# A hybrid decoder layer: early window transfers and gate projections dealt over the sample units

## The chip, the cores and the metric

The kernel runs on one core of a Trainium2 chip. The metric is the device time of one execution in microseconds, the median of the runs shown. TensorE (PE) does the matrix products, ScalarE (ACT) and VectorE (DVE) the element-wise work, GpSimd (POOL) some element-wise work and the issue of gathers, SyncE (SP) the issue of most transfers.

## The reference

One inference step of a decoder layer for a prompt of 512 tokens and a batch of 8 single-token samples with 2048 past positions. What matters here, cut down:

```python
h = rms_norm(x, ln1_g)
u2, q, kc, vc, ks, vs, kw, vw, ng, g_conv, g_attn = split(h @ w_in)      # D_MODEL = 1024
u = u2[..., :1024] * sigmoid(u2[..., 1024:])
c_out = silu(layer_norm(depthwise_conv(u, width=31))) @ w_conv_pw
# attention: 16 heads, 4 key/value heads; three branches, each softmax(q k - alibi) v, weighted by gates from ng:
#   compressed blocks; 16 selected blocks of 64 rows; sliding window of 512 rows
# prompt: causal over 512 tokens. sample: 2048 cached rows in pages (cache_slc_kv), 512 rows of state_win_kv
m = sigmoid(g_conv) * c_out + sigmoid(g_attn) * a_out
x = x + m @ w_out
x = x + square(relu(rms_norm(x, ln2_g) @ w_up)) @ w_down
y = rms_norm(x, lnf_g)
```

The outputs are the layer's result for prompt and samples and the updated key/value and convolution state.

## The kernel before

Prompt and samples are worked on together: activations lie transposed, 128 channels by 520 columns (512 prompt tokens and 8 samples), in two halves of 256 and 264 columns. Each matrix product is done as three matmuls of split operands, high by high, high by low and low by high, so a projection tile of 128 output channels costs 8 x 3 x 2 = 48 matmuls in `dense` (L435 to L437). `wload` fetches its weights in two pieces of 256 KB over SP's queue (L400) into three rotating raw buffers, casts the high part on ACT (L412) and subtracts for the low part (L414).

The work goes in stages. First come the norm, projections and prompt attention (`attend`, to about 500 us). Beside it run the pooled past of the samples (`pool_cache`, buffers `cg`), the convolution (`conv_taps`, L1099 on DVE) and first projections (`u_proj`) as fillers. Then comes the sample stage (`Sample`), then the merge with `w_conv_pw` (`merge`, beside `residual`, which loads x again), then the output projection and the feed-forward part to the end.

The sample stage has ten columns of two units each, in the order of SORDER: columns 8 and 9 are the sliding window of samples 0 to 3 and 4 to 7, columns 0 to 7 the selected past of one sample each. A unit reads two row sets (tile `sg`, 128 x 2048 numbers, 1 MB each): a window transfer from `state_win` (L900) or a gather (L317), both issued on POOL. A unit transposes its rows (L925), copies them on ACT (L926), forms scores (L929), takes them over on DVE (L934) and ACT (L936), transposes them (L938), multiplies them with the values (L941) and copies the result (L944). Six `sg` buffers rotate, so a row set can be fetched once the unit three back is through L941. They lie in memory that prompt attention gives free. `finish` joins the units; its large product is L1013.

Gate projections run beside this as fillers: `gate_attn` (eight tiles, the first during prompt attention) and `gate_conv` (eight tiles). From the second on, an attention gate may go as soon as prompt attention has been written out; conv gates 0 to 5 follow, and gates 6 and 7 (HELD) are held until the last unit's scores (L929) are issued. A hold is `issue_after`: the matmuls stand behind the named instruction in TensorE's order.

The order on each engine is fixed when the program is built. Generators write instructions in the ratio of their weights (`run`; W_S for the sample units, W_D2 for the gates), with a priority (`urgent` raises it, `lowered` lowers it). A planner, which simulates a time line, then puts on each engine the ready instruction of highest priority. An engine then works in that order: what waits holds up all that stands behind it on its engine, and so does a transfer on SP's or POOL's queue. Memory is given out in areas from the left and from the right; a tile waits for the tiles that lay there before.

In `residual` (L1463) the loads of x go to an area on the right that takes over memory of the sample stage; the loads of the merge's weights follow on the same SP queue.

Of the kernel before, what the change touches and what calls it, by code (L numbers as in the profile page):

```python
# [17 lines left out]
P = 128  # L18
# [12 lines left out]
EPS = 1e-6  # L31
FILL = 3000
TL_S = True
KTS_B, SG_B, U1, Y1, UP1 = 5, 6, 2, 4, 4
SC_D = (1, 2)
PS1 = {"pss": 2, "pst": 2, "pso": 1, "psp": 1}
PS2 = {"psx": 2, "psy": 3, "psn": 1}
# [18 lines left out]
U_EARLY = (32, 48, 56, 74)  # L56
POOL_P, PROJ_D = True, False
GA1, W_G, PRI_G = 1, 2, 500
W_P, W_D, W_S, W_D2, W_C, W_U = 55, 55, 120, 8, 300, 20
WIN_E = lambda nc: nc.gpsimd  # L60
XF = False
LOW_D = 6
# [1 line left out]
SQ_D, WARM, EARLY = (), 20, 2  # L64
NORDER = "q0 q1 s02 m0 m1 t0 t1 q2 q4 q3 s25 m4 m2 t4 m3 t2 t3"
PACK = 5000
HELD = 6
SYNC = mybir.DependencyInfo(mybir.DependencyClass.Sync, mybir.DependencyReason.DATA)
BIG = 1e30
FLOOR = 1e25  # L70
# [60 lines left out]
def hybrid_layer(ctx: ExitStack, tc: tile.TileContext, I, C, O):  # L131
# [297 lines left out]
    def dense(wh, wl, aH, aL, evac, n=P, ins=None, halves=(0, 1)):  # L429
        for hf in halves:  # L430
            c = HS[hf]
            ps = psd()[:, :c.stop - c.start]
            for k in range(KD):
                with after(ins):
                    pe.matmul(ps[:n], wh[:, k, :n], aH[:, k, c], start=(k == 0), stop=False)  # L435
                pe.matmul(ps[:n], wh[:, k, :n], aL[:, k, c], start=False, stop=False)  # L436
                end = pe.matmul(ps[:n], wl[:, k, :n], aH[:, k, c], start=False, stop=(k == KD - 1))  # L437
            ends.append(end)
            evac(hf, c, ps)
# [434 lines left out]
    class Sample:  # L874
# [10 lines left out]
        def first(self):  # L885
# [4 lines left out]
            dve.tensor_copy(self.sn.rearrange("p s b -> p b s"), ps)  # L890
            yield

        def cached(self, b, q):
            g = self.gp.tile([P, 4, 512], F32, name="sg", bufs=SG_B)
            gather(cache_s, gix[:, b, q:q + 1], g)
            return g

        def window(self, b):
            g = self.gp.tile([P, 4, 512], F32, name="sg", bufs=SG_B)
            WIN_E(nc).dma_start(g, state_win[b].rearrange("(p r) f -> p r f", r=4))  # L900
            return g

        def attend(self, col):
# [8 lines left out]
            for e in range(2):  # L912
# [3 lines left out]
                for i in range(2):  # L916
# [4 lines left out]
                    for h in range(2):  # L921
                        kt = sp.tile([P, 512], F32, name="kts", tag="kts", bufs=KTS_B)
                        ps = psx([P, 4, P])
                        for r in range(4):
# [3 lines left out]
                    yield  # L928
                run_ = packed([lambda n=n: pe.matmul(pq[32 * n:32 * n + 32], Qz[:, n % 2, bs[n // 2]], kts[n], start=True, stop=True,  # L929
                                              skip_group_check=True) for n in range(4)], *cps)  # L930
                if col == SORDER[-1] and e == 1:
                    UY["scored"] = run_
                t = sp.tile([P, 512], F32, name="tq", tag="kts", bufs=KTS_B)
                dve.tensor_tensor_reduce(out=t, in0=pq, in1=bias.rearrange("p r k -> p (r k)"), scale=1.0,  # L934
                                         scalar=FLOOR, op0=OP.add, op1=OP.min, accum_out=st[:, 0, at:at + 1])
# [283 lines left out]

    def gate_attn():  # L1220
        for k in range(KD):
            while ("attn", k) not in built or (k >= GA1 and "late" not in UY):
                yield
            wh, wl = wload(w_in, [(C_GA + P * k, P)])
            ga = temp("ga")

            def ev(hf, c, ps):
                act.activation(ga[:, c], ps, AF.Tanh, scale=0.5)
                p0, n = pcols(hf)
                a = attnT[:, k, p0:p0 + n]  # L1230
                dve.scalar_tensor_tensor(a, ga[:, p0:p0 + n], 1.0, a, op0=OP.add, op1=OP.mult)
            dense(wh, wl, hH, hL, ev)
            dve.tensor_scalar(sA[:, k], ga[:, NP_:], 1.0, None, op0=OP.add)
            yield

    def gate_conv():
        for k in range(KD):
            while k >= HELD and "scored" not in UY:
                yield
            wh, wl = wload(w_in, [(C_GC + P * k, P)])  # L1240
            gc = GC[k] = gcp.tile([P, T], F32, name="gc", bufs=KD)
            dense(wh, wl, hH, hL, lambda hf, c, ps: act.activation(gc[:, c], ps, AF.Tanh, scale=0.5),
                  ins=UY["scored"] if k >= HELD else None)
            yield

    def merge(cH, cL, mH, mL):
# [117 lines left out]
    def pool_conv():  # L1364
        yield from pool_cache(plp2)
        last = UY["cs"]
        for b in range(NB):
            with tc.issue_after(last.ins):
                last = nc.sync.dma_start(o_win_s[0, b, 0:511].rearrange("l j h d -> l (j h d)"), state_win[b, 1:512])
            yield  # L1370
        pl2_s.close()
        while NKV - 1 not in KV:
            yield
        UY["mo"], mo = area("mo", side="right")
        UY["msk"], UY["oC"] = mo.tile([P, NB, 32], F32, name="msk"), mo.tile([P, 2, 256], F32, name="oC")
        cs, cp_ = area("cmpp", side="right")
        yield from urgent(sample_cmp(cp_, UY["msk"], UY["oC"]), PRI_C)
        cs.close()
# [75 lines left out]
    m2s, m2 = area("m2")  # L1454
    mH = m2.tile([P, KD, T], F32R, name="mH")
    mL = m2.tile([P, KD, T], F32R, name="mL")
    gs, gp = area("gp", side="right")

    def residual():
        for j in range(5):  # L1460
            n = P if j < 4 else NB
            xt = gp.tile([P, D], F32, name="xr", tag="p4", bufs=2)
            nc.sync.dma_start(xt[:n], xp[P * j:P * j + P] if j < 4 else xs)  # L1463
            for kk in range(2):
                ps = pst([P, 4, P])
                for k in range(4):
                    c = (4 * kk + k) * P
                    pe.transpose(ps[:, k, :n], xt[:n, c:c + P], ident[:n, :n])
                act.copy(x1[:, 4 * kk:4 * kk + 4, P * j:P * j + n], ps[:, :, :n])
            yield  # L1470
    run((merge(cH, cL, mH, mL), 8), (residual(), 4))
    gs.close()
    gc_s.close()
    UY["st"].close()
    UY["mo"].close()
    uy1_s.close()
    xgH = hp.tile([P, KD, T], F32R, name="xgH", tag="H")
# [160 lines left out]
```

## Time and profile before

| | us |
|---|---|
| median of 3 runs | 1187.1 |
| lowest and highest run | 1181.41, 1187.92 |
| the profiled execution, its time | 1196.35 |
| the profiled execution, its span | 1194.5 |
| TensorE busy in the span | 1135.8 (95%) |
| VectorE busy | 747.4 (63%) |
| ScalarE busy | 542.6 (45%) |
| GpSimd busy | 253.0 (21%) |

The profile is one execution. The page gives each engine's busy time in the span; matmuls overlap, so a busy TensorE is one that has work, and its idle time is read from the windows. The granted clock is the share of full speed that TensorE was given, a mean over the stretch of its two levels, 1.2 and 2.4 GHz. "Idle before" in brackets is the time an engine stood before an instruction and what released it.

### The profile page before, as it was taken

To read this page: it belongs to the slowest core of one execution; us is meant where nothing else is said; L and a number is where in the kernel's file an instruction comes from. 1 tells how busy PE (TensorE), PEld (TensorE's weight loads), DVE (VectorE), ACT (ScalarE), POOL (GpSimd) and SP (SyncE) were. 2 spreads that over 40 slices of the span, in tenths; PEclk is the share of its full clock that TensorE was granted. 3 is DMA by queue.
4 is the path that set the end of the run, shared out by engine and by line. 5 is a ranking of instruction groups with operands and counts; after the bars stand their busy time and mean duration, and the time that the engine had idled before them with its cause. 6 is when DMAs were issued, how large, how long until landed. Compare 5 with 4: busy or idle time off the path is not lost.

```text
span 1194.5 us, 24755 instructions
## 1 busy us (share of the span) xinstructions
PE 1135.8 (95%) x9755; PEld 1006.2 (84%) x9755; DVE 747.4 (63%) x1773; ACT 542.6 (45%) x1384; POOL 253.0 (21%) x284
## 2 busy tenths in 40 slices
PE   6899998999999999999999699999999999999996
PEld 6777974776677677888898579999999999999996
DVE  4341455486899799989976666556543443443476
ACT  5352465535542655345657734344431431431454
POOL 2345445343474012003322300000000000000012
PEclk9899999999998999999999999999999999999998
DMA  6646555173364851657787624333333333333354
GB/s 175 179 135 206 166 150 168 39 209 99 115 177 118 292 153 37 203 199 251 281 304 270 221 89 126 89 89 107 90 98 97 89 89 89 97 98 90 89 166 136
DMA packets 188364, 175.46 MB, mean 147 GB/s; under 512 B 35277, under 2 KB 171021, under 8 KB 182984
## 3 DMA queue, kind: packets, MB, share of 16 engines
q1 hardware_dynamic: 172472, 96.54, 28.5%
q0 software_dynamic: 15296, 76.55, 18.4%
q8 instruction: 77, 1.26, 0.4%
q10 hardware_dynamic: 480, 0.79, 0.3%
q14 instruction: 39, 0.32, 0.1%
HBM read 167.58 MB, written 14.80 MB: 153 GB/s over the span
## 4 chain that ended last, share of the span: by engine, by line
PE 73%; DVE 13%; DMA 8%; issue 2%; ACT 2%; POOL 1%; SPq 1%; DVEq 0%; ACTq 0%; POOLq 0%
PE psd L435 18%; PE psd L436 18%; PE psd L437 18%; DVE y L1099 5%; DMA wraw<-in_w_in_dram 3%; PE psx L925 3%; PE psp L772 3%; DMA sg<-in_cache_slc_kv_dram,gix 2%; PE pss L679 2%; DMA cg<-in_cache_cmp_kv_dram,gic 2%; PE pso L744 2%; PE pst L739 2%; DVE pp L643 2%; DVE pp L728 2%; PE psy L941 2%
## 5 line engine op out<-in xcount | busy, mean ns | idle before, releaser
L412 ACT CAST wh<-wraw 128x512 fp32r<-128x512 f32 x282 | 162.3, 617 | 296.4 <-PE psd L436 219.6
L435 PE MATMUL psd<-hH,wh 128*128 128x264 f32 (+2 forms) x848 | 249.9, 296 | 4.4 <-ACT hH L348 2.2
L437 PE MATMUL psd<-hH,wl 128*128 128x264 f32 (+2 forms) x848 | 245.7, 292 | 0.2 <-POOL wl L414 0.2
L436 PE MATMUL psd<-hL,wh 128*128 128x264 f32 (+2 forms) x848 | 245.0, 290 | 0.4 <-DVE hL L349 0.4
L414 DVE TENSOR_TENSOR wl<-wraw,wh 128x512 fp32r<-128x512 f32 (+1 forms) x230 | 154.5, 707 | 77.5 <-ACT wh L412 73.2
L1099 DVE SCALAR_TENSOR_TENSOR y<-u,cwT,y 128x512 f32<-128x512 f32 x240 | 192.7, 803 | 4.5
L435 PEld LDWEIGHTS psd<-hH,wh 128*128 128x128 f32 (+1 forms) x848 | 160.5, 190 | 13.5 <-issue 7.1
L437 PEld LDWEIGHTS psd<-hH,wl 128*128 128x128 f32 (+1 forms) x848 | 159.9, 189 | 7.8 <-issue 6.6
L436 PEld LDWEIGHTS psd<-hL,wh 128*128 128x128 f32 (+1 forms) x848 | 160.6, 190 | 4.5 <-issue 3.2
L435 PE MATMUL psd<-xgH,wh 128*128 128x264 f32 (+1 forms) x512 | 144.8, 283 | 0.0
L436 PE MATMUL psd<-aT,wh 128*128 128x264 f32 (+1 forms) x512 | 144.7, 283 | 0.0
L435 PE MATMUL psd<-aT,wh 128*128 128x264 f32 (+1 forms) x512 | 144.7, 283 | 0.0
L437 PE MATMUL psd<-aT,wl 128*128 128x264 f32 (+1 forms) x512 | 144.7, 283 | 0.0
L437 PE MATMUL psd<-xgH,wl 128*128 128x264 f32 (+1 forms) x512 | 144.5, 282 | 0.0
L436 PE MATMUL psd<-xgL,wh 128*128 128x264 f32 (+1 forms) x512 | 144.2, 282 | 0.0
L1577 POOL TENSOR_TENSOR attnT<-attnT,gfb 128x512 f32<-128x512 f32 (+1 forms) x8 | 10.5, 1331 | 493.7 <-DVE sqd L1572 493.7
L647 ACT ACTIVATE pp<-pp,st 128x256 f32<-128x256 f32 (+3 forms) x128 | 71.2, 557 | 84.1 <-DVE st L643 77.3
L436 PEld LDWEIGHTS psd<-xgL,wh 128*128 128x128 f32 x512 | 96.6, 189 | 0.0
L437 PEld LDWEIGHTS psd<-xgH,wl 128*128 128x128 f32 x512 | 96.5, 188 | 0.0
L435 PEld LDWEIGHTS psd<-aT,wh 128*128 128x128 f32 x512 | 96.3, 188 | 0.1
L435 PEld LDWEIGHTS psd<-xgH,wh 128*128 128x128 f32 x512 | 96.3, 188 | 0.0
L436 PEld LDWEIGHTS psd<-aT,wh 128*128 128x128 f32 x512 | 96.2, 188 | 0.0
(380 smaller groups left out, 2262.3 us busy)
## 6 DMA issues: line engine op xcount, KB each, us to landing
wraw<-in_w_in_dram SPq DMA_DIRECT2D x88, 256.0 KB
wraw<-in_w_down_dram SPq DMA_DIRECT2D x80, 256.0 KB
wraw<-in_w_up_dram SPq DMA_DIRECT2D x64, 256.0 KB
sg<-in_state_win_kv_dram POOLq DMA_DIRECT2D x8, 1024.0 KB
out_dram<-in_state_win_kv_dram SPq DMA_DIRECT2D x8, 1022.0 KB
wraw<-in_w_in_dram SPq DMA_DIRECT2D x32, 128.0 KB
wraw<-in_w_conv_pw_dram SPq DMA_DIRECT2D x16, 256.0 KB
wraw<-in_w_out_dram SPq DMA_DIRECT2D x16, 256.0 KB
```

The source lines that it names most:

```text
L412: act.copy(a, raw[:, :, :o])
L414: (low or (dve if 2 <= len(loaded) < LOW_D else LOW[0])).tensor_tensor(b, raw[:, :, :o], f32(a), op=OP.subtract)
L435: pe.matmul(ps[:n], wh[:, k, :n], aH[:, k, c], start=(k == 0), stop=False)
L436: pe.matmul(ps[:n], wh[:, k, :n], aL[:, k, c], start=False, stop=False)
L437: end = pe.matmul(ps[:n], wl[:, k, :n], aH[:, k, c], start=False, stop=(k == KD - 1))
L643: v = dve.tensor_tensor_reduce(out=ph, in0=ps, in1=bias, scale=slope[e], scalar=FLOOR, op0=OP.add, op1=OP.min, accum_out=st[:, 0, e, i:i + 1])
L647: act.activation(ph, ph, AF.Exp, scale=-1.0, bias=st[:, 0, e, i:i + 1], accum_out=st[:, 1, e, i:i + 1])
L679: mms.append(lambda ps=ps, e=e, i=i, xi=xi, nk=nk: pe.matmul(ps, rq(e, i), KR[g, e, r][:, 32 - xi:32 + nk], start=True, stop=True))
L728: dve.tensor_scalar(ph, ph, rr[:, e, i:i + 1], None, op0=OP.mult)
L772: packed([lambda r=r, j=j, i=i: pe.matmul(po[32 * i:32 * i + 32, j], wpa[:, 2 * rh + r, j], gs[i][:, r, 256 * j:256 * j + 256], start=(rh ...
L925: pe.transpose(ps[:, r], g[:, r, P * h:P * h + P], ident)
L1099: prev = dve.scalar_tensor_tensor(yk, u[:, w:w + NP_], cwT[:, k, w:w + 1], yk, op0=OP.mult, op1=OP.add)
```

## The change

- Two of the six `sg` buffers go, and a new area `sgx` of three such buffers is opened on the right, after the pooled past is done, in memory that its tiles (`cg` and others) have left: seven buffers in all. The windows of samples 0, 1 and 2 are fetched into it at that place in the program, before `sample_cmp`. `rows` then takes three row sets from `sgx` and four from the old area in turn.
- The area stays until the merge is done, and `residual` loads x into it (three buffers) in place of an area of its own.
- The memory for DMA descriptors goes from 16384 to 8192 bytes, which makes room for 8 KB more per partition.
- Every unit's last score matmul is kept in `UY["scored", n]`. Attention gate k (k from 1) is held until unit GA_AT[k] is scored, and conv gate k until unit GC_AT[k]. The hold for the end (HELD) goes.
- The generator weight W_D2 of the gates goes from 8 to 40.

```diff
-KTS_B, SG_B, U1, Y1, UP1 = 5, 6, 2, 4, 4
+SGX, KTS_B, SG_B, U1, Y1, UP1 = 3, 5, 4, 2, 4, 4
-W_P, W_D, W_S, W_D2, W_C, W_U = 55, 55, 120, 8, 300, 20
+W_P, W_D, W_S, W_D2, W_C, W_U = 55, 55, 120, 40, 300, 20
-HELD = 6
+GA_AT, GC_AT = (0, 1, 3, 5, 7, 8, 9, 10), (11, 12, 13, 14, 15, 16, 17, 18)
...
+        def rows(self):
+            self.n = n = getattr(self, "n", SGX - 1) + 1
+            if n % (SGX + SG_B) < SGX:
+                return UY["sgx"].tile([P, 4, 512], F32, name="sg", tag="sgx", bufs=SGX)
+            return self.gp.tile([P, 4, 512], F32, name="sg", bufs=SG_B)
+
         def cached(self, b, q):
-            g = self.gp.tile([P, 4, 512], F32, name="sg", bufs=SG_B)
+            g = self.rows()
             gather(cache_s, gix[:, b, q:q + 1], g)
...
         def window(self, b):
-            g = self.gp.tile([P, 4, 512], F32, name="sg", bufs=SG_B)
+            if UY["pre"]:
+                return UY["pre"].pop(0)
+            g = self.rows()
...
-                if col == SORDER[-1] and e == 1:
-                    UY["scored"] = run_
+                UY["scored", 2 * SORDER.index(col) + e] = run_
...
     def gate_attn():
-            while ("attn", k) not in built or (k >= GA1 and "late" not in UY):
+            while ("attn", k) not in built or (k >= GA1 and ("scored", GA_AT[k]) not in UY):
...
-            dense(wh, wl, hH, hL, ev)
+            dense(wh, wl, hH, hL, ev, ins=UY["scored", GA_AT[k]] if k >= GA1 else None)
...
     def gate_conv():
-            while k >= HELD and "scored" not in UY:
+            while ("scored", GC_AT[k]) not in UY:
...
-                  ins=UY["scored"] if k >= HELD else None)
+                  ins=UY["scored", GC_AT[k]])
...
+        sgx_s, UY["sgx"] = area("sgx", side="right")
+        UY["sgx_s"], UY["pre"] = sgx_s, []
+        for b in range(SGX):
+            g = UY["sgx"].tile([P, 4, 512], F32, name="sg", tag="sgx", bufs=SGX)
+            WIN_E(nc).dma_start(g, state_win[b].rearrange("(p r) f -> p r f", r=4))
+            UY["pre"].append(g)
         cs, cp_ = area("cmpp", side="right")
...
-    gs, gp = area("gp", side="right")
...
-            xt = gp.tile([P, D], F32, name="xr", tag="p4", bufs=2)
+            xt = UY["sgx"].tile([P, 4, 512], F32, name="xr", tag="sgx", bufs=SGX).rearrange("p r f -> p (r f)")[:, :D]
...
-    nc = bacc.Bacc("TRN2", target_bir_lowering=False, num_devices=1, dynamic_dma_scratch_size=16384)
+    nc = bacc.Bacc("TRN2", target_bir_lowering=False, num_devices=1, dynamic_dma_scratch_size=8192)
```

## Rows read from the trace of the kernel before

**Rows 1.** Stages: length, PE, PEld, DVE, ACT, POOL, PEclk, DMA share, GB/s.

```profile
430.00:500.00 70.00, 68.98 (x573) 55.48 (x571) 67.73 (x183) 32.33 (x98) 10.83 (x16) 1.00 0.31 87
500.00:510.00 10.00, 10.00 (x110) 9.66 (x106) 8.40 (x15) 3.78 (x8) 1.75 (x4) 1.00 0.89 318
510.00:530.00 20.00, 18.23 (x154) 15.32 (x157) 14.88 (x28) 8.22 (x19) 0.46 (x1) 0.91 0.42 138
530.00:590.00 60.00, 59.38 (x659) 53.34 (x649) 57.63 (x102) 34.89 (x79) 22.13 (x26) 1.00 0.78 264
590.00:660.00 70.00, 69.27 (x762) 60.91 (x761) 47.74 (x87) 44.99 (x100) 20.01 (x21) 1.00 0.82 283
660.00:690.00 30.00, 21.03 (x244) 14.37 (x243) 19.62 (x38) 20.87 (x41) 6.84 (x6) 0.89 0.56 206
690.00:710.00 20.00, 18.45 (x218) 15.49 (x217) 11.54 (x63) 4.73 (x11) 0.00 (x0) 1.00 0.32 107
710.00:720.00 10.00, 9.38 (x57) 8.60 (x58) 8.36 (x16) 6.44 (x14) 0.00 (x0) 0.83 0.35 105
800.00:900.00 100.00, 100.00 (x834) 99.84 (x834) 55.24 (x114) 41.59 (x89) 0.00 (x0) 1.00 0.33 96
```

**Rows 2.** Waits of TensorE, 440 to 720 us: total us, times, longest.

```profile
PE psx L925 <- DMA sg<-in_cache_slc_kv_dram,gix: 8.0, 5, 2.8
```

**Rows 3.** Chain that ended last, 498 to 725 us: start us, us, what.

```profile
502.48 13.38 DMA wraw<-in_w_in_dram
...
560.84 6.46 DMA sg<-in_cache_slc_kv_dram,gix
...
583.97 0.99 PE psy L929 x8
584.97 1.03 PE psx L925 x8
...
586.35 1.01 PE psy L941 x32
...
675.91 8.03 DMA sg<-in_cache_slc_kv_dram,gix
...
704.73 4.25 DMA wraw<-in_w_conv_pw_dram
```

**Rows 4.** Time line of POOL: start us, us, engine, line, what, idle before.

```profile
439.91 2.10 POOL L730 TENSOR_SCALAR pp<-pp,st 128x128 f32<-128x128 f32 x4 [14.62 <-DVE st L655]
...
477.01 0.61 POOL L900 DMA_DIRECT2D sg<-in_state_win_kv_dram  x1
...
499.66 2.09 POOL L900 DMA_DIRECT2D sg<-in_state_win_kv_dram  x4 [3.74 <-PE pso L744]
...
539.82 1.02 POOL L317 DMA_INDIRECT sg<-in_cache_slc_kv_dram,gix  x1 [7.89 <-PE psy L941]
```

**Rows 5.** DVE's time line: scores of units 0, 7, 18, 19; convolution's last step.

```profile
521.99 0.69 DVE L934 CUSTOM_DVE_ANT_0 tq<-psy,sb_win 128x512 f32<-128x512 f32 x1
...
585.43 0.68 DVE L934 CUSTOM_DVE_ANT_0 tq<-psy,bm 128x512 f32<-128x512 f32 x1
...
678.07 0.69 DVE L934 CUSTOM_DVE_ANT_0 tq<-psy,bm 128x512 f32<-128x512 f32 x1
...
687.38 0.70 DVE L1210 SCALAR_TENSOR_TENSOR y<-th,v 128x520 f32<-128x520 f32 x1 [1.31 <-ACT th L1205]
689.38 0.69 DVE L934 CUSTOM_DVE_ANT_0 tq<-psy,bm 128x512 f32<-128x512 f32 x1 [1.30 <-PE psy L929]
```

**Rows 6.** ACT's time line: attention gates 1 and 2 end; merge's weights.

```profile
478.30 0.38 ACT L1228 ACTIVATE ga<-psd 128x264 f32<-128x264 f32 x1
...
508.98 0.39 ACT L1228 ACTIVATE ga<-psd 128x264 f32<-128x264 f32 x1
...
708.25 1.36 ACT L412 CAST wh<-wraw 128x512 fp32r<-128x512 f32 x2 [3.16 <-DMA wraw<-in_w_conv_pw_dram]
```

**Rows 7.** Waits of SP's queue, 640 to 740 us.

```profile
SPq L1463 <- PE psy L1013: 46.1, 1, 46.1
```

More of the change, by code (lines that the diff above doesn't have):

```diff
@@ L1471, in hybrid_layer @@
     run((merge(cH, cL, mH, mL), 8), (residual(), 4))
-    gs.close()
     gc_s.close()
     UY["st"].close()
+    UY["sgx_s"].close()
     UY["mo"].close()
```

## The prediction

> **What bounds the kernel now.** I read the page first (TensorE is busy for nearly the whole span), then the busy time by stage to see where it is not. The stages before 430 us and after 720 us are left alone by the change: in the feed-forward stage TensorE is busy 100.00 of 100 us at full clock with 834 matmuls, 0.120 us each [rows 1]. So a microsecond counts only if TensorE stands or runs slow between 430 and 720 us. The same rows give that ledger as stretch minus busy time: 1.0 us lost in 430 to 500, 0 in 500 to 510, 1.8 in 510 to 530, 0.6 in 530 to 590, 0.7 in 590 to 660, 9.0 in 660 to 690, 1.6 in 690 to 710 and 0.6 in 710 to 720: 15.3 us of idle. Below full clock the loss is (1 - granted clock) times the stretch: 0.09 x 20 = 1.8, 0.11 x 30 = 3.3 and 0.17 x 10 = 1.7, together 6.8 us. All that any change here can win is 22 us.
>
> The waits of TensorE say what the 9.0 us are: its transposes of sample rows (L925) wait 8.0 us for gathered row sets [rows 2]. The fillers had run out; the last row set takes 8.03 us in the chain [rows 3]. A second hole, at 515 us, is a weight load that took 13.38 us [rows 3], issued 3 us after four 1 MB window transfers had been issued in one go at 499.66 [rows 4].
>
> **Prices.** A projection tile is 3 x 8 x 2 = 48 matmuls: 48 x 0.120 = 5.8 us [rows 1], and 0.52 MB of weights. A sample unit (half a column, two row sets, 20 units in all) is, by the chain's pieces, two groups of L925 at 1.03, L929 at 0.99, L941 at 1.01 [rows 3], and L938 with half a group's transposes, 0.5: 4.6 us.
>
> **The early windows.** Three of eight window transfers leave the stretch after 477 us and go to where the pooled-cache tiles have been read for the last time. The data rate of 430 to 500 us is 87 GB/s, share 0.31 [rows 1], so 3.1 MB fit in. Three issues at about 0.6 us [rows 4] go into POOL's queue ahead of the scalings of prompt attention (L730); POOL stands idle 14.62 us before one of these [rows 4], so 1.8 us costs nothing; if a window were queued there before its memory is free, the scalings behind it wait too, up to the few us until that memory is read. I take 0, between -1 and 5.
> The Trainium skill, "SBUF — State Buffer", section "A bandwidth-pool intuition that's wrong", says that a transfer issued by GpSimd can stretch from about 620 to 3100 ns beside DVE copies, because descriptors wait for a shared port. Worked out from that figure, an estimate: 2.5 us more per row set. DVE is busy 67.73 of 70 us in 430 to 500 and 57.63 of 60 in 530 to 590 [rows 1], yet a gather there took 6.46 us where the last one, with DVE two thirds busy, took 8.03 [rows 3]: the trace does not show it. By the rule the 13 row sets up to unit 7 could take up to 32 us more, which is the slower rival (c); by the rows, nothing.
> What the early windows bring: the first unit, scored at 521.99 [rows 5], can start when prompt attention frees the PSUM banks, about 500, so it is scored near 507. Fewer windows are in flight beside the 13.38 us weight load: its stall and the low clock behind it (1.8 + 1.8 us) mostly go.
>
> **Seven row buffers for six.** A unit's gathers wait for L941 three units back; with seven, one of the two waits for four back. Worth a little slack, priced at 0. The descriptor memory halves; before, at most six row sets were in flight, after it seven. No row shows a full descriptor memory; the nearest is the issue itself, four in 2.09 us without a pause [rows 4]. I take 0; the far end is that each of 40 issues doubles, 40 x 0.5 = 20 us on a POOL that is idle two thirds of the stretch [rows 1], so at most a few us reach TensorE; a gain has no way to come from it.
>
> **The dealt gates.** The generator's weight (W_D2, 8 to 40) only sets how soon a gate is written into the program behind its unit and adds no instruction: 0. Two attention gates (k = 1 and 2), which filled TensorE until 478.30 and 508.98 [rows 6], are now held until units 1 and 3 are scored: 11.6 us of filler leaves the stretch up to 509. The last pair of first-projection tiles can move up into it (11.6 us), if its buffers allow. From 500 to the score of unit 7 TensorE then has 8 x 4.6 = 37, gates 1 to 3 = 17, half of the last pair = 6: 60 us. The transfers of that stretch are 13 row sets and about six tiles, 13.6 + 3.1 = 16.7 MB; at the 283 GB/s of 590 to 660 [rows 1] that is 59 us from 499, then about 6 us from landing to score: 564. At 264 GB/s it is 568, at 318 (500 to 510) 558 [rows 1]. I take 565 for the score of unit 7 (585.43 before [rows 5]), with 6 us of TensorE idle instead of 0.6.
> From there each unit has one gate beside it (k = 4 to 7 of attention, then conv 0 to 6): 11 x (4.6 + 5.8) = 114 us, plus some 6 for the convolution's sums, which interleave: unit 18 is scored at about 685, against 678.07 [rows 5], but with two more gates done. Per unit 2.6 MB in 10.4 us is 250 GB/s, below the 283 already sustained, so no gather should be waited for: 9.0 us of idle and 3.3 us of clock go, about 1 us stays.
>
> **The tail.** Before, two conv gates (11.6 us) were kept for the end; the last unit is scored at 689.38 [rows 5] and the merge starts behind the weight cast of 708.25 [rows 6], near 710. After, only conv gate 7 is left, about half of it for the tail. What is late next is the merge's weights. SP had the residual's loads (L1463) ahead of them, and they waited 46.1 us for L1013, the last product of the sample stage [rows 7]. Now the residual's rows lie in the window buffers, freed a unit or two earlier, and the merge's weights wait only for the last unit's L941. I put that 5 us after the score (reading 0.69, exponent, transpose, copy, product), and the load with casts at 4.25 [rows 3] + 1.36 [rows 6] + some 2 for issue and subtraction. So the merge starts 12.6 us after the last score, of which TensorE has about 4.5 us of its own and 3 of gate 7: 5 us idle, and about 2 us of low clock after it. The convolution's last step ends at 687.38 + 0.70 [rows 5], and its split needs some 5 us more: 693, not the bound.
>
> **Sum.** Lost after: 1 (430 to 500) + 6 (to unit 7) + 1 (to unit 18) + 5 (tail) + 0.5 (elsewhere) + 2 (clock) = 15.5; before 22.1: a gain of 6.6. By times instead: last score near 688 (unit 18 at 685 plus about 4.6, less overlap), merge at 701 against 710, a gain of 9, and 1.5 more if its first tile does not repeat 1.7 us of low clock: 10.5. I take the middle, 8.6 us. The profiled execution has a span of 1194.5 in 1196.35 us; it would become 1187.8. The runs' median lies 9.25 lower; the same difference puts it at 1187.1 - 8.6 = **1178.5 us**.
>
> **Rivals.** (a) *TensorE alone bounds the early units.* If the row sets come at 318/0.89 = 357 GB/s, the rate of 500 to 510 at full share [rows 1], they are there by 546 and unit 7 is scored at 500 + 60 = 560: 5 us better, 1173.5. Against it: no stretch of 60 us shows more than 283. Chance 0.15.
> (b) *The hole moves.* The last first-projection pair cannot take the place of the held gates, because its output buffer waits for DVE's convolution and DVE is 97% busy there [rows 1]; TensorE then idles 5.8 us for gate 1 and some 2 for gate 2 before 509. The gain falls to 8.6 - 7.8: 1186.3. For it: DVE's load. Against it: only the last write of such a tile needs that buffer. Chance 0.25.
> (c) *Slower: the early units stay gather-bound.* Place: units 0 to 7, which have three gates instead of about five for filler. If TensorE, which works in a written order, stands before transposes whose rows are late, and unit 7 is scored at its old 585.43, then 11 gates still come behind it: 585 + 120 + the last unit, and the merge starts 20 us later than forecast, 11 later than before: 1198. It decides from unit 7 later than 565 + 9 = 574; every us behind that is a us lost. For it: each unit needs 2.1 MB in 8 us, 263 GB/s beside weights, about what 530 to 590 shows at share 0.78 [rows 1]. Against it: the windows' head start of 3 MB. Chance 0.18.
> (d) *The windows do not come early* (POOL takes them where it did before): unit 0 starts near 515 with the gates still held; about half of (c): 1190. Against it: POOL's idle [rows 4]. Chance 0.07.
> The forecast has the remaining 0.35, with 1174 to 1184 as its own range.
>
> **Range and chances.** About 0.5%, 6 us, is what a measurement of this kernel tells from no change: faster means below 1181.2, slower above 1193.0. Forecast (nearly 0.3 of 0.35) and (a) give faster 0.46, and a twelfth of the rest 0.03: 0.49. (c) gives most of slower, 0.14, and (d) and the unknown ends of POOL's queue 0.04: 0.18. The same: 0.33. The range runs from 1169, half of the remaining idle gone, to 1195, most of (c).
>
> **What would show it.** Right: window transfers on POOL before 450 us; unit 0 scored before 510 and unit 7 before 570; no wait above 1 us of L925 for gathers after 600; the residual's loads no longer waiting for L1013; merge at about 701 with a hole of some 5 us ahead of it. Wrong: idle TensorE between 450 and 510 (b), L925 waiting for gathers in 510 to 570 (c), or a merge that waits for the convolution.

## The result, and the profile after

The changed kernel took 1194.18 us in the median of 7 runs (1192.1 to 1196.75), the kernel before 1187.92 in 7 runs beside it (1181.41 to 1192.92): ratio 1.0064, 95% interval 1.0041 to 1.0088. It is slower by 6.3 us; 1178.5 was forecast. The profiled execution has a span of 1192.4 us. The ratios below leave out three single executions that ran far slower than their neighbours (1380.72 us in e2, 6131.11 in e4, and 3627.24 in e9, its profiled one); the medians of these three kernels are over all runs and lie 0.1 to 0.3 us higher for it.

The stages of the changed kernel, with the columns of [rows 1]:

```profile
430.00:500.00 70.00, 59.63 (x479) 38.96 (x478) 65.80 (x174) 32.93 (x97) 13.64 (x21) 0.90 0.35 123
500.00:510.00 10.00, 10.00 (x111) 9.07 (x110) 3.52 (x7) 4.44 (x11) 2.36 (x3) 1.00 0.90 335
510.00:530.00 20.00, 20.00 (x236) 17.95 (x238) 9.36 (x21) 12.07 (x28) 4.88 (x5) 1.00 0.82 287
530.00:590.00 60.00, 60.00 (x664) 54.98 (x657) 58.07 (x93) 34.37 (x77) 20.07 (x19) 1.00 0.80 277
590.00:660.00 70.00, 70.00 (x792) 61.05 (x791) 49.11 (x111) 40.66 (x91) 16.29 (x22) 1.00 0.74 250
660.00:690.00 30.00, 29.66 (x283) 26.66 (x283) 24.00 (x71) 15.57 (x31) 0.00 (x0) 1.00 0.39 103
690.00:710.00 20.00, 15.26 (x125) 15.05 (x124) 17.72 (x31) 13.01 (x25) 0.00 (x0) 0.97 0.21 62
710.00:720.00 10.00, 10.00 (x77) 10.00 (x77) 6.89 (x14) 5.35 (x11) 0.00 (x0) 0.88 0.18 51
```

From 500 to 690 TensorE is idle for 0.3 us, where [rows 1] shows 12 us. The part that the windows were to mend is mended. But 430 to 500, which had 68.98 of 70 at clock 1.00 [rows 1], now has 59.63 at a granted clock of 0.90: 10.4 us idle and 6 us of slow clock. And 690 to 710 is still short by 4.7 us.

GpSimd's time line of the changed kernel (start, duration, what): the windows do go out early, and the first gather goes out at 497.87 instead of 539.82 [rows 4].

```profile
421.37 0.61 POOL L1387 DMA_DIRECT2D sg<-in_state_win_kv_dram  x1
433.13 1.06 POOL L1387 DMA_DIRECT2D sg<-in_state_win_kv_dram  x2 [11.15 <-issue]
497.87 1.18 POOL L317 DMA_INDIRECT sg<-in_cache_slc_kv_dram,gix  x1 [0.30 <-PE psy L945]
```

VectorE's time line, the scores of units 0, 7, 18 and 19 and the convolution's last step; they answer to [rows 5]:

```profile
490.01 0.69 DVE L941 CUSTOM_DVE_ANT_0 tq<-psy,sb_win 128x512 f32<-128x512 f32 x1
547.65 0.69 DVE L941 CUSTOM_DVE_ANT_0 tq<-psy,bm 128x512 f32<-128x512 f32 x1
643.23 0.68 DVE L941 CUSTOM_DVE_ANT_0 tq<-psy,bm 128x512 f32<-128x512 f32 x1
651.10 0.68 DVE L941 CUSTOM_DVE_ANT_0 tq<-psy,bm 128x512 f32<-128x512 f32 x1
712.38 0.70 DVE L1217 SCALAR_TENSOR_TENSOR y<-th,v 128x520 f32<-128x520 f32 x1
```

The last unit is scored 38 us earlier than in [rows 5], the convolution's last step comes 25 us later (30 earlier and 32 later than in the second profile of the kernel before, e1 below; the first was late ahead of this stage). What happened to the convolution stands in ScalarE's time line, where each dense product is read out (tb and ah are the two products of a first projection, ga an attention gate):

```profile
444.38 0.38 ACT L1064 ACTIVATE tb<-psd 128x264 f32<-128x264 f32 x1
499.91 0.39 ACT L1235 ACTIVATE ga<-psd 128x256 f32<-128x256 f32 x1 [0.87 <-PE psd L437]
507.83 0.39 ACT L1057 ACTIVATE ah<-psd 128x256 f32<-128x256 f32 x1
509.81 1.14 ACT L412 CAST wh<-wraw 128x512 fp32r<-128x512 f32 x2 [1.11 <-PE psd L436]
510.86 0.38 ACT L1235 ACTIVATE ga<-psd 128x264 f32<-128x264 f32 x1
```

After projection 4 (444.38) no dense product is read out for 55 us. Then gate 1 comes (499.91), and only behind it projection 5 (507.83), though no hold is on projection 5. The order in which a pair of weight tiles and an accumulator bank are handed out is the order in the source: gate 1, projection 5, gate 2, projection 6, gates 3 to 5, projection 7. There are two pairs and two banks. Gate 1 takes a pair and both banks (one for each half), and it may start only behind unit 0, which needs the end of prompt attention. So in the trace gate 1 begins on TensorE at 494.32, behind the last product of prompt attention (done at 483.9), and projection 5 behind gate 1, at 503.40. In the kernel with the row sets alone (e4 below) gate 1 begins at 439.2 and projection 5 at 451.39, between the attention products, the last of which is done at 493.9.

SyncE's queue stands as well: it issues four pieces of weights from 433.20 to 446.8 and the next at 511.18, where the kernel with the row sets alone issues twelve between 431 and 488. First a small constant (L883) waits 32.2 us for memory of prompt attention, then the weight load behind it 30.7 us until an earlier one has been split (L414), which needs a free weight tile (total us, times, longest):

```profile
SPq L400 <- DVE wl L414: 74.9, 6, 30.7
SPq L883 <- DVE pt L742: 32.2, 1, 32.2
```

The queue is not what held projection 5 back. The weights of its first product were cast and split by 446.4, and no other weights were cast before 509.81; its first matmul still ran at 503.40, behind gate 1:

```profile
443.35 1.12 ACT L412 CAST wh<-wraw 128x512 fp32r<-128x512 f32 x2
445.14 1.27 DVE L414 TENSOR_TENSOR wl<-wraw,wh 128x512 fp32r<-128x512 f32 x2
503.40 0.37 PE L435 MATMUL psd<-hH,wh 128*128 128x256 f32 x1
```

TensorE's own waits in 430 to 500 name none of this:

```profile
PE pst L739 <- POOL pp L730: 3.3, 3, 1.8
PE pst L739 <- ACT pt L742: 2.2, 2, 2.0
PE pso L744 <- DVE pt L742: 2.0, 3, 0.9
```

These are prompt attention's own steps (mask, copy, normalise). They ran before too, but with dense work between them TensorE waited 1.0 us for them there (e1); that work is what is gone. A hole of this kind is not found under the wait that it shows, but under the work that is missing there.

Late projections make late taps (the convolution's multiply-and-add steps on VectorE), and the merge waits at its start. The first merge product of the changed kernel:

```profile
709.35 0.58 PE L435 MATMUL psd<-cH,wh 128*128 128x256 f32 x1 [4.74 <-ACT gc L1249]
```

It waited for the last conv gate's read-out (gc), which ScalarE did at 708.91, behind some of the convolution's tanh and split (cH) steps. That the late convolution makes this wait is not shown: e12 below waits 5.2 us at the same place with its convolution done at 681.

### The profile page after: what moved, and what is told of

Same layout as the page of the kernel before. It is cut to its first block, busy times and chain, and to the rows that moved or that the text cites. A ratio compares the mean times of both kernels' runs of the same rounds, so it can differ in the third digit from the quotient of the medians.

```text
span 1192.4 us, 24768 instructions
## 1 busy us (share of the span) xinstructions
PE 1134.0 (95%) x9755; PEld 1006.5 (84%) x9755; DVE 745.4 (63%) x1773; ACT 545.7 (46%) x1384; POOL 249.9 (21%) x284
## 4 chain that ended last, share of the span: by engine, by line
PE 75%; DVE 11%; DMA 8%; ACT 2%; issue 2%; POOL 1%; SPq 1%; DVEq 0%; POOLq 0%; ACTq 0%
PE psd L435 19%; PE psd L436 19%; PE psd L437 19%; DVE y L1106 5%; DMA cg<-in_cache_cmp_kv_dram,gic 4%; PE psx L933 3%; DMA wraw<-in_w_in_dram 3%; PE psp L772 2%; PE pss L679 2%; PE psy L948 2%; PE psy L937 2%; PE pso L744 2%; PE pst L739 2%; DVE pp L643 1%; DVE pp L728 1%
## 5 line engine op out<-in xcount | busy, mean ns | idle before, releaser
L414 DVE TENSOR_TENSOR wl<-wraw,wh 128x512 fp32r<-128x512 f32 (+1 forms) x230 | 155.0, 711 | 96.3 <-ACT wh L412 92.2
L1106 DVE SCALAR_TENSOR_TENSOR y<-u,cwT,y 128x512 f32<-128x512 f32 x240 | 196.4, 818 | 4.9
```

Source lines behind the costliest of these rows:

```text
L414: (low or (dve if 2 <= len(loaded) < LOW_D else LOW[0])).tensor_tensor(b, raw[:, :, :o], f32(a), op=OP.subtract)
L1106: prev = dve.scalar_tensor_tensor(yk, u[:, w:w + NP_], cwT[:, k, w:w + 1], yk, op0=OP.mult, op1=OP.add)
```

## Experiments

Theory 1, from the traces above: a held attention gate closes the rotation of weight tiles and banks to the projections behind it; TensorE loses its filler in prompt attention, the convolution is late, the merge waits. Against it: the seven row sets and early windows cost by themselves (rival 2); sixteen dealt gates leave too little filler or too much for the end (rival 3); the new order of the weight tiles costs, held or not (rival 4); the halves of the change hurt only together (rival 5).

Ratios are to runs of the kernel before on the same chip, with 95% intervals. Behind the ratios stands a sum from each kernel's one profiled execution: the idle time of TensorE in 430 to 720, and what it lost to a granted clock below 1 (busy time times 1 minus the clock, in the eight stretches of [rows 1]). "Read-out" is when ScalarE first reads out projection 4's second product (tb), a common mark at the start of the stretch; "rest" is the execution's time less read-out, idle and clock.

| kernel | median us | ratio, interval | profiled us | read-out | idle | clock | rest |
|---|---|---|---|---|---|---|---|
| before, first profile | 1187.9 | | 1196.35 | 441.66 | 15.3 | 5.5 | 733.9 |
| before, second profile (e1) | 1188.3 | | 1188.30 | 435.43 | 16.4 | 2.9 | 733.5 |
| changed | 1194.2 | 1.0064 (1.0041 to 1.0088) | 1194.18 | 437.72 | 15.5 | 7.6 | 733.4 |
| e4 row sets alone | 1180.2 | 0.9928 (0.9903 to 0.9954) | 1180.03 | 435.83 | 6.4 | 3.4 | 734.4 |
| e7 dealing alone | 1205.7 | 1.0138 (1.0110 to 1.0167) | 1205.70 | 433.97 | 25.0 | 12.4 | 734.4 |
| e5 row sets, one hold | 1200.8 | 1.0113 (1.0089 to 1.0136) | 1203.90 | 441.19 | 19.9 | 7.0 | 735.8 |
| e10 changed, gate 1 free | 1187.8 | 0.9997 (0.9975 to 1.0019) | 1186.04 | 435.50 | 9.7 | 5.8 | 735.0 |
| e6 changed, no attention holds | 1181.2 | 0.9938 (0.9915 to 0.9962) | 1185.26 | 441.51 | 5.9 | 4.4 | 733.5 |
| e2 changed, projections first | 1181.2 | 0.9934 (0.9909 to 0.9959) | 1178.81 | 433.16 | 7.3 | 5.0 | 733.4 |
| e11 the same, gates free | 1181.0 | 0.9936 (0.9911 to 0.9962) | 1179.60 | 434.52 | 5.8 | 2.9 | 736.3 |
| e3 gates free, handed out fast | 1186.3 | 0.9975 (0.9956 to 0.9995) | 1183.25 | 438.68 | 14.1 | 1.5 | 728.9 |
| e12 gates free, handed out slowly | 1188.5 | 0.9984 (0.9954 to 1.0015) | 1188.50 | 437.24 | 12.6 | 3.9 | 734.7 |
| e8 third weight pair | 1195.6 | 1.0063 (1.0042 to 1.0083) | 1196.65 | 435.24 | 17.6 | 12.0 | 731.8 |

The last column stays within 732 to 736 (729 in e3) while the profiled times spread over 27 us: where two executions differ, they differ by TensorE time in this stretch, or by a shift ahead of it. Such a shift cannot be put down to an edit: the two profiles of the kernel before differ by 6.2 us there.

**e1, the kernel before again** (no edit).

> The kernel before, unchanged, for a second profile. The first one ended some 9 us above the median of its times and was already 3.9 us late at 400 us, where both kernels run the same work; this one should end near 1188, with the first merge matmul near 704 to 706 instead of 710.19 and everything between 430 and 690 as in the first profile, shifted by about 4 us. If it ends near 1196 again, the first profile stands as it is and the two traces can be laid on one another without a shift.

1188.3 us, span 1186.5; its merge starts at 702.60, and 430 to 500 has 69.03 of 70 at clock 1.00. 6.2 of the 7.6 us by which the first profile's merge was later (710.19) lie ahead of the stage. The changed kernel's merge start (709.35) is 6.8 us later than here, of which 2.3 lie ahead of the stage (read-out) and 4.5 in it.

```profile
430.00:500.00 70.00, 69.03 (x599) 56.77 (x596) 66.55 (x176) 31.14 (x95) 12.54 (x19) 1.00 0.36 106
660.00:690.00 30.00, 22.88 (x269) 18.18 (x268) 19.79 (x67) 17.54 (x35) 4.80 (x5) 0.94 0.39 141
702.60 0.39 PE L435 MATMUL psd<-cH,wh 128*128 128x256 f32 x1 [2.15 <-ACT cH L1216]
```

Idle time and clock loss together are 1.0 us here and 16.3 in the changed kernel in 430 to 500, 14.2 and 0.3 in 500 to 690, 4.1 and 6.4 in 690 to 720. So the loss is the hole and 2 us at the merge, less what the windows mended: some 4 us of the 6.3 by which the medians differ. Where the rest lies is open; it is smaller than the shifts ahead of the stage. Over the whole stretch the changed kernel is not idle for longer (15.5 against 16.4 us); what makes it slower here is the clock (7.6 against 2.9).

**e2, projections first.**

```
-while ("attn", k) not in built or (k >= GA1 and ("scored", GA_AT[k]) not in UY):
+while ("attn", k) not in built or (k >= GA1 and (("scored", GA_AT[k]) not in UY or len(U) < KD)):
```

> The changed kernel, with one edit: the attention gates 1 to 7 are emitted only after all eight first projections, so that they stand behind projections 5 to 7 in the rotation of weight tiles and accumulator banks; windows, seven row sets, hold points and weights stay. Theory 1 (a held attention gate sits in one of the two weight tiles and blocks the projections behind it, the convolution is late, the merge waits for it): the DVE wait for u tiles near 500 to 530 and 590 to 620 goes, the last tap ends at 615 to 630 (changed kernel 653.9, before 617.5), the merge starts near 697 to 703, and the time is 1178 to 1185. Rival 2 (the seven row sets and early windows themselves cost): the taps come early and the time stays at 1191 to 1196. Rival 3 (sixteen gates behind unit scores leave too much for the end): the taps come early, but the gates still fill PE up to 705 to 710 and the time is 1187 to 1193.

1181.16. The hole is gone, the last tap ends at 604 and the merge starts at 692.84, both earlier than expected. Its first stage:

```profile
430.00:500.00 70.00, 70.00 (x589) 58.36 (x588) 67.57 (x173) 32.85 (x98) 9.22 (x18) 1.00 0.44 148
```

Every hold of the change is still in it; only their place in the rotation differs. Theory 1 holds, rival 2 falls.

**e3, attention gates free** (not held; handed out as soon as prompt attention ends, at the change's weight of 40).

```
-while ... (k >= GA1 and ("scored", GA_AT[k]) not in UY):
+while ... (k >= GA1 and "late" not in UY):
...
-    dense(wh, wl, hH, hL, ev, ins=UY["scored", GA_AT[k]] if k >= GA1 else None)
+    dense(wh, wl, hH, hL, ev)
```

> The changed kernel, with the attention gates 1 to 7 no longer held behind a unit's score (emitted and run as in the kernel before); the convolution gates stay dealt out, windows and row sets stay. Theory 1: the projections 5 to 7 come as in the kernel before (last one read out by about 540), the last tap ends near 615, the early holes between 440 and 480 shrink because gates 1 and 2 fill them again, and the time is 1178 to 1186; if the early fill is what matters, this is faster than the kernel with projections first. Rival 2: 1191 to 1196. Rival 3: sample units 0 to 4 start later again (first score near 500), TensorE is full to 705 and the time is 1186 to 1191.

1186.3, just above the range of theory 1 (1178 to 1186) and inside that of rival 3 (1186 to 1191), and slower than e2. Without holds nothing stops the gates: seven read-outs of gates stand between projections 5 and 6 (495 to 525), projection 7 ends at 581, the taps at 630. A gate that is not held delays a projection too, but TensorE works meanwhile: 67.78 of 70 us in 430 to 500.

**e4, row sets alone** (the change less its dealing: attention gates as in e3, two conv gates held, weight 8).

```
-W_D2 = 40
+W_D2 = 8
...
-while ("scored", GC_AT[k]) not in UY:
+while k >= HELD and ("scored", 19) not in UY:
...
-    ins=UY["scored", GC_AT[k]])
+    ins=UY["scored", 19] if k >= HELD else None)
```

> The kernel before with the memory part of the change alone: three row sets fetched in prompt attention, seven in all, half the descriptor scratch, residual rows in the freed sets; attention gates free and only two convolution gates held, weights as in the kernel before. Theory 1: no matmul waits for a row set, units start near 500, the taps end near 615, and the time is 1178 to 1187, at least 5 us under the changed kernel. Rival 2: the row sets cost by themselves (SyncE's or POOL's queue, or the scratch), and the time is 1191 to 1197. Also told apart: with the early gates spent before 600, is there filler left for the late sample units; if not, idle time appears at 600 to 690 and the time comes to 1186 to 1190.

1180.17. Unit 0 is scored at 508.11, unit 7 at 565.10, the last at 673.66, the merge starts at 693.35. TensorE's waits for row sets in 430 to 720 sum to 1.7 us (first its stage at the hole's place, then that wait):

```profile
430.00:500.00 70.00, 69.62 (x605) 57.44 (x604) 67.53 (x176) 32.79 (x98) 11.09 (x19) 1.00 0.40 128
PE psx L934 <- DMA sg<-in_cache_slc_kv_dram,gix: 1.7, 2, 1.2
```

**e5, one hold added to e4.**

```
-dense(wh, wl, hH, hL, ev)
+dense(wh, wl, hH, hL, ev, ins=UY["scored", 0] if k == 1 else None)
```

> The kernel with the row sets alone (1180.2), and one thing added: attention gate 1, and no other, may start only behind the score of sample unit 0, as in the changed kernel; the order in which weight tiles are handed out is the same to the last tile. Theory 1 (the held gate closes the rotation to the projections behind it): the hole at 430 to 500 comes back, PE busy about 60 of 70 with a granted clock near 0.9, projection 5 is read out after 505 instead of near 466 to 477, taps end some 15 us or more later, and the time rises by 6 to 10 us, to 1186 to 1190. Rival 3 (it is the number of gates held, above all 3 to 5 ahead of projection 7, and the gates piled up at the end): one hold costs 0 to 2 us, 1180 to 1182.

1200.84: one hold on one gate, of the 5.8 us of TensorE that the prediction counts for a gate, costs 20.7 us (1.9% by the two ratios). Stages of e5:

```profile
430.00:500.00 70.00, 60.48 (x460) 40.26 (x458) 65.76 (x178) 31.39 (x93) 13.04 (x19) 0.90 0.35 127
710.00:720.00 10.00, 4.40 (x31) 4.19 (x31) 6.18 (x10) 6.02 (x12) 0.00 (x0) 0.79 0.33 100
```

ScalarE in e5 reads out gate 1 at 498, projection 5 behind it:

```profile
447.83 0.38 ACT L1065 ACTIVATE tb<-psd 128x264 f32<-128x264 f32 x1
498.20 0.39 ACT L1236 ACTIVATE ga<-psd 128x256 f32<-128x256 f32 x1
506.93 0.39 ACT L1058 ACTIVATE ah<-psd 128x256 f32<-128x256 f32 x1
```

and in e4, without the hold, between attention products:

```profile
442.46 0.38 ACT L1065 ACTIVATE tb<-psd 128x264 f32<-128x264 f32 x1
447.86 0.38 ACT L1236 ACTIVATE ga<-psd 128x256 f32<-128x256 f32 x1
457.33 0.36 ACT L1058 ACTIVATE ah<-psd 128x256 f32<-128x256 f32 x1
```

This is the cleanest pair: one line of the source differs. The expectation (6 to 10 us) had counted the idle time alone; the trace adds 6 us of clock in the hole and a merge that waits 5.6 us, with the taps ending at 635 instead of 610.

**e6, the changed kernel without attention holds, order kept.**

```
-dense(wh, wl, hH, hL, ev, ins=UY["scored", GA_AT[k]] if k >= GA1 else None)
+dense(wh, wl, hH, hL, ev)
```

> The changed kernel with the holds of attention gates 1 to 7 taken off, while the order in which weight tiles are handed out stays that of the changed kernel (gate 1 ahead of projection 5, gate 2 ahead of 6, gates 3 to 5 ahead of 7); convolution gates dealt out as there. Theory 1: gates 1 and 2 fill 440 to 500 again, the hole goes (PE 68 to 70 of 70 at clock 1.0), projection 7 comes 20 to 45 us earlier than 597 to 621, the time is 1182 to 1187, near the 1186.3 of the kernel with free gates, whose order puts five gates ahead of the last projections. Rival 4 (the order of the weight tiles alone is the cost, held or not): the hole may close, but the taps still end past 645, and the time is 1191 to 1195.

1181.21, a little better than expected, and no hole. The order that the change made costs nothing by itself; rival 4 falls.

```profile
430.00:500.00 70.00, 69.80 (x580) 56.41 (x579) 68.48 (x186) 32.87 (x99) 10.66 (x19) 1.00 0.33 104
```

**e7, dealing alone** (the kernel before, six row sets, with the change's hold points and weight).

```
-HELD = 6
+GA_AT, GC_AT = (0, 1, 3, 5, 7, 8, 9, 10), (11, 12, 13, 14, 15, 16, 17, 18)
...
+dense(wh, wl, hH, hL, ev, ins=UY["scored", GA_AT[k]] if k >= GA1 else None)
```

> The kernel before with the dealing of the gates alone (hold points and weight of the change; six row sets, no early windows, scratch as before). Theory 1: both halves of the change are there to be added: rows alone gave -0.7%, dealing should cost what the change lost on top of that, so the hole at 430 to 500 is there with PE near 58 to 60 of 70, it is longer since unit 0 comes after 510, and the time is 1197 to 1206. Rival 5 (the two halves hurt only together, since the early units rob the projections of their place): 1185 to 1191, no hole.

1205.67. Its hole is the deepest:

```profile
430.00:500.00 70.00, 53.70 (x374) 34.38 (x376) 63.60 (x168) 27.56 (x84) 11.30 (x20) 0.78 0.32 114
```

The halves add up: 0.72% gained by the row sets and 1.38% lost by the dealing make 0.66%, against 0.64% measured for both. Rival 5 falls.

**e8, a third pair of weight tiles** (two early row sets instead of three pay for it).

```
-SGX, KTS_B, SG_B, U1, Y1, UP1 = 3, 5, 4, 2, 4, 4
+SGX, KTS_B, SG_B, U1, Y1, UP1 = 2, 5, 4, 2, 4, 4
...
-wt_s, wts = area("wts", bufs=2)
+wt_s, wts = area("wts", bufs=3)
```

> The changed kernel with a third pair of weight tiles, paid for with one of the three early row sets (two early, six in all). It tells apart which of two rotations closes behind the held gate: the two weight tiles or the two accumulator banks of the dense products. If the weight tiles alone: projection 5 passes gate 1, the hole at 430 to 500 falls under 3 us, time 1182 to 1188. If the banks close it as well: projection 5 still follows gate 1 (read out after 505), its weights are merely cast earlier, PE is about 60 of 70 in 430 to 500, time 1191 to 1197.

1195.56, and the hole stays, with projection 5 read out from 506 on:

```profile
430.00:500.00 70.00, 59.06 (x434) 38.19 (x435) 61.88 (x167) 31.90 (x94) 13.69 (x20) 0.85 0.37 131
```

On TensorE projection 5 still begins behind gate 1 (500.28 behind 493.68). More weight tiles alone do not open the rotation. That fits the changed kernel, where projection 5's first weights were ready and waited. That the two banks by themselves would close the rotation follows from the program, and was not tried: prompt attention uses the other six.

**e9 and e12, the row sets with the conv gates dealt out** (e3 at weight 8, so with e4's order of weight tiles).

> The row sets with the convolution gates dealt out behind units 11 to 18 as in the change, and the attention gates free and handed out slowly, as in the kernel before (weight 8, not 40). The orders of the weight tiles are those of the kernel with row sets alone. Theory 1: only held attention gates cost; dealing the convolution gates is worth between -3 and +2 us against the row sets alone (1180.2), so 1177 to 1182, and the 4 to 5 us of the kernel with free gates at weight 40 (1186.3) came from the five attention gates that stood ahead of the last projections. Rival 3 (the dealing of convolution gates costs): 1185 to 1188 again.

1188.03, ratio 0.9990 (0.9967 to 1.0013): theory 1's number missed. The kernel was run again for a profile of the stage.

> The kernel with row sets, free attention gates and dealt convolution gates once more, since its first profile fell into a stretch with a granted clock of 0.16 and shows nothing after 600 us. Its times (1188.0) were 7 us above the kernel with row sets alone, which theory 1 did not expect. If rival 3 holds here, the loss is after 600: the held convolution gates leave idle time or clock loss of 5 us or more in 590 to 720 that the kernel with row sets alone (2.1 us idle in 660 to 690, 1.2 in 690 to 710) does not have, and the merge starts near 700 rather than 693. If the first times were chance, this one is at 1179 to 1183 and its merge starts at 692 to 695.

1188.52; the time was no chance. Stages of e12:

```profile
590.00:660.00 70.00, 66.74 (x732) 56.01 (x731) 46.81 (x84) 46.96 (x103) 21.49 (x20) 1.00 0.78 278
690.00:710.00 20.00, 14.80 (x119) 14.00 (x108) 11.68 (x32) 7.04 (x14) 0.00 (x0) 0.83 0.18 54
```

In 590 to 660 e4 has 70.00 of 70. Here, with the attention gates read out by 594, TensorE is idle for 3.3 us, and at the end the merge waits 5.2 us for the last gate's read-out, which ScalarE does behind the split's casts. That is what rival 3 expected, so it has a part in e12: e4 and e12 differ by the dealing of the conv gates alone, and 1180.2 became 1188.5. But e6 deals the conv gates out in the same way, has its attention gates done just as early (600), and takes 1181.2. So the dealing of the conv gates is not enough to explain e12, and the weight is not either (e3 has 40, e12 has 8). For e3 the place of the projections is enough: e11 below is e3 with one condition more, the first projections ahead of the gates, and takes 1181.0, with its last tap at 608 instead of 630. For e12, whose projections and taps are in time (taps end at 613, in e6 at 616), it stays open what makes the 7 us to e6 and e11.

**e10, gate 1 alone free in the changed kernel** (k > GA1 instead of k >= GA1 at its ins).

> The changed kernel with the hold taken off attention gate 1 alone; gates 2 to 7 and the convolution gates stay held, the order of the weight tiles stays. Theory 1: gate 1 and projection 5 fill prompt attention to about 480 to 490, then gate 2 closes the rotation; the hole shrinks from 10.4 us to 2 to 5 us, the clock stays up for most of 430 to 500, projection 6 is read out near 525 to 545, and the time is 1182 to 1188, most of the 13 us that all holds cost. Rival 4 (it is the order, or the last projections behind gates 3 to 5): 1191 to 1195.

1187.78; 6.4 of the 13 us that all the attention holds cost come back by freeing one gate, half and not most:

```profile
430.00:500.00 70.00, 66.52 (x601) 49.25 (x604) 68.67 (x179) 37.46 (x107) 13.22 (x21) 1.00 0.43 142
```

Projection 6 then waits behind held gate 2 (read out at 518 to 538) and projection 7 comes at 578 to 604.

**e11, projections first and gates free** (e3 with e2's condition: no attention holds; the weight is the change's 40, not the 8 that the expectation names).

> A try at a version better than both: row sets, first projections ahead of attention gates 1 to 7, those gates free, convolution gates dealt out, weight 8. Theory 1: no gate can close the rotation in front of a projection; TensorE has filler in each stretch and bounds the stage, so the time is that of the three good kernels so far (1180 to 1181), at best 3 us under it: 1177 to 1181. If it is above 1184, filler runs out in the last units (idle time in 590 to 690).

1180.97, no better than e2, e4 and e6. All four beat the kernel before by 0.6 to 0.7% and the changed one by 1.1 to 1.2% (13 to 14 us), and cannot be told from one another. Of what is left in them, 9 to 12 us by the table, half to three quarters lies in 660 to 710, where the merge takes over.

## Why the prediction was wrong, step by step

- *The ledger of 22 us.* Its clock part was taken from whole stretches, which counts the idle time in them twice. From busy time it is 5.5 us instead of 6.8, together 20.8, and 19.3 in the second profile.
- *The windows come early; unit 0 near 507, unit 7 at 565.* Right as a mechanism: 508.11 and 565.10 in e4, where nothing else changed. In the changed kernel they are 490.01 and 547.65: without dense work between its products, prompt attention was done at 483.9 instead of 493.9.
- *No gather waited for after 600; sets that arrive in time.* Right in what it forecast: 1.7 us in e4, none named among the changed kernel's waits. But the prediction gave this gain (9.0 us idle and 3.3 of clock) to the dealt gates, and e4 has it without them. Gathers landed in a median of 7.3 us in 530 to 590 of the changed kernel, with VectorE busy for 58.07 of 60 us, and of 7.4 in 590 to 660, with 49.11 of 70. So rival (c), whose mechanism was late gathers, falls although its sign was right. The stretching beside VectorE's copies that the Trainium skill describes in "SBUF — State Buffer", section "A bandwidth-pool intuition that's wrong", did not show; VectorE's work in 530 to 590 was mostly the convolution's multiply-and-add (44.1 us), not copies, so that case is not put to the test here.
- *"The last pair of first-projection tiles can move up into it (11.6 us), if its buffers allow."* This is the step that failed. I looked at the output buffer of the projection and not at what stands ahead of it: the held gate keeps a weight pair and both banks, so nothing of the dense work can pass it. In 430 to 500, where 1 us was expected to be lost, 16.3 were (10.4 idle and 6.0 of clock).
- *From unit 7 on one gate beside each unit; unit 18 at 685; only conv gate 7 left for the tail.* Wrong in the changed kernel: unit 18 is scored at 643.23, and at the last score (651.10) one of the sixteen half products of the conv gates had been read out (at 647.50). A hold sets the earliest place of a gate, not its place; the units ran ahead and the gates piled up behind them. By itself this cost little, since TensorE was idle for only 0.3 us in 500 to 690.
- *Rival (b), the hole moves.* Closest: the hole is where (b) put it, priced 7.8 us with a time of 1186.3. Its cause was another (u's output buffer, which waits for VectorE; e6 reads projection 5 out from 463 to 482 with VectorE as busy), and it missed the clock and the late convolution. As a result it ended near no change where the changed kernel lost 6.3.
- *The generator's weight, 8 to 40: 0.* Not contradicted: e2, e6 and e11 keep 40 and are as fast as e4 with 8.
- *Convolution 693, "not the bound".* Off by 20 us in the changed kernel: its last step ends at 713.1, behind the merge's start, and on ScalarE its tanh and split stand between the last read-outs. Whether it bounds the merge there is open, as said above. In e4, where projections are in time, the last step ends at 671.0 and it was right.
- *The tail: merge at 701 with a hole of 5 us.* 709.35 with 4.74. In e1 the merge before stood at 702.6, so 701 was a smaller gain than it looked; with row sets alone it is 693.35. The residual's loads no longer wait for the sample stage's last product, as forecast: instead of 46.1 us [rows 7] one waits 5.5 for a unit's L948, and the fourth 10.6 at 717, when the merge is under way:

```profile
SPq L1475 <- PE psd L436: 10.6, 1, 10.6
SPq L1475 <- PE psy L948: 5.5, 1, 5.5
```

The row sets alone gained 8.9 us, near the 8.6 forecast for the whole change. That is chance: the forecast's gain was to come from the dealt gates and the tail as well. The dealing, priced as a gain, cost 16 us alone (1.38%) and 14 beside the row sets (the changed kernel against e4); its attention holds make 13 of them (against e6).

## What to carry to other kernels

A hold on one instruction group is a hold on everything that is handed buffers after it. Before pricing one at the work that it moves, list the rotating buffers it takes (weights, accumulator banks), what stands behind it in each, and what that work feeds; then put held work last in the rotation, or give it buffers of its own in every rotation that it takes part in (not tried here; more weight tiles alone did not help). And where a stretch is full of another stage's short latencies, its filler is worth more than its own length: here 5.8 us of gate, held, cost 20.7.

## What the runs showed of the hardware

The clock's part of a hole was larger than expected. In the changed kernel TensorE was busy for 7.38 us in 440 to 450; in 450 to 460 and 470 to 480 the granted clock was 0.68 and 0.67 in the mean, part of the time at 1.2 GHz instead of 2.4, and in 460 to 470 it was back at 1.00:

```profile
440.00:450.00 10.00, 7.38 (x57) 4.03 (x55) 10.00 (x28) 5.96 (x16) 0.00 (x0) 0.98 0.50 153
450.00:460.00 10.00, 7.87 (x47) 5.14 (x47) 9.57 (x40) 4.99 (x22) 3.43 (x5) 0.68 0.05 19
460.00:470.00 10.00, 8.18 (x50) 4.55 (x48) 9.10 (x32) 5.16 (x18) 0.00 (x0) 1.00 0.01 2
470.00:480.00 10.00, 7.33 (x29) 3.75 (x29) 8.07 (x16) 1.07 (x2) 3.75 (x5) 0.67 0.30 106
```

Over the 70 us of 430 to 500, 3.5 us idle cost no clock in e10, while e11 and e12 lost 1.4 with no idle time at all. 9.5 and 10.4 us idle cost 6.0 each (e5 and the changed kernel), 10.9 cost 8.9 (e8) and 16.3 cost 11.8 (e7). So the few microseconds idle were nearly free, and the long holes cost another 0.6 to 0.8 us for each us idle; between 3.5 and 9.5 no run lies.
